# A decoder trunk's mixer: two 64-token halves in one product, decay levels by halves, one product for the upper scores

## Chip, cores and metric

The kernel runs on one core of a Trainium2 chip. The metric is the device time of one execution in microseconds (us); the median of three runs before the change is 965.5 us (965.27 to 966.09). The core's engines work side by side and meet through semaphores: PE (matrix products; PEld are its loads of the stationary operand), DVE (elementwise), ACT (activations and copies), POOL (small helper operations), and SP, which issues the DMAs.

## What is computed

The input is x, 256 tokens of 1024 values. Two layers follow each other. A layer is a half-step gated FFN, a token mixer, and a second half-step FFN, each with a residual and a layer norm. The mixer has two groups: trailing means over 2, 4, 8 and 16 tokens, and a gated linear recurrence (HGRN2) of four heads with 128 dimensions. The change concerns the recurrence:

```python
log_f = jnp.logaddexp(jnp.log(lb), jnp.log1p(-lb) + jax.nn.log_sigmoid(f_raw))
k = (1.0 - lb) * jax.nn.sigmoid(-f_raw)
# per head, state S (128 x 128), token t:
#   S_t = diag(f_t) S_{t-1} + (1 - f_t) outer v_t ;  o_t = S_t^T q_t
# within a chunk, with b = cumsum(log_f) over its tokens:
rel = b[:, :, :, None, :] - b[:, :, None, :, :]
decay = jnp.exp(jnp.where(causal, rel, -jnp.inf))
scores = jnp.einsum('bhtd,bhsd,bhtsd->bhts', q_c, k_c, decay)
o_intra = jnp.einsum('bhts,bhsv->bhtv', scores, v_c)
```

The score of two tokens s < t is thus a sum over the 128 dimensions of q times k times a decay of that dimension, and the decay is exp of the sum of the log gates between s and t.

## The kernel before

The 256 tokens are two halves of 128 (`hf` 0 and 1). Each weight arrives as fp32, is cast to a rounded high part on ACT and reduced to a low part on DVE (`halves`, L101), and a product of two fp32 operands is three products of parts (`mm3`, L95). In the FFN, `GT` (L282) makes the products with the high parts 512 columns wide and those with the low parts of the weights 256 columns wide.

The order on PE is written out: PE runs in program order (L88), and the small products of the mixer are dealt in between the large projections by `later`, a queue whose clock ticks once for each `mm3`. `later(n, fn)` issues `fn` n ticks on. ACT, DVE and POOL are ordered by the planner, by priority; the casts and subtractions of weights have a priority lowered by 400 (`BEHIND`), so they fill gaps.

The mixer (L519) projects five blocks (gate f, q, v, output gate, pooling input) for both halves in turn. For the recurrence:

- `post_f` (L542) turns the projected gate into log gates `ls` (128 tokens x 512 dimensions) and splits them into high and low parts `lh` and `ll` on all 128 tokens (L560 to L563).
- `decays(hf, h)` (L619), one call a head, forms sums of log gates over spans of tokens as products with a constant 0/1 matrix `cumM` of 1024 columns a half: for each of two groups of 512 columns one product with `lh` (L629) and one with `ll` (L630), accumulated in one PSUM bank, then an exponential on ACT into the tile `E` (L631).
- With the second head of a pair, DVE multiplies the decays by transposed q or k (`kT`, `qT`), 14 operations by `mul` (L637) and a copy of every second q on POOL (L636). Two of the 14 write `A256`, the operands of the product that joins the two halves of 128 tokens (`cross`).
- `grams(hf, hp)` (L651), one call a pair of heads, multiplies the decayed k by the decayed q: blocks of 128, 32 and 8 tokens, each cut into four quarters, three cuts a level, and a further operand for neighbouring tokens. For each level and head there is one fp32 product (L657). Its valid parts go into the tile `scores`, a part of `Pm`: three copies on ACT for the level of 128 (L665), masked copies on DVE for 32 and 8 (L668, L671). Fp32 products appear as two instructions each in the trace.
- `output` (L689) multiplies the scores by v.

After `post_q` of a half, its transposes come four ticks on; `decays` of head h follows at `lag + 2h` ticks, `grams` at `lag + 9` and `lag + 14`, and `cross` at `lag + 17`, with `lag` 7 in layer 0 and 11 in layer 1 (L584 to L590). The PSUM pool `psa` has four banks, which `decays` and `grams` share.

The constants come from `_constants` (L807) and are loaded once, in the first FFN (`load_consts`, L216).

Of the kernel before, what the change touches and what calls it, by code (L numbers as in the profile page):

```python
# [28 lines left out]
ALPHA = (2.0 * DEPTH) ** 0.25  # L29
LN_EPS = 1e-5  # L30
RMS_EPS = 1e-6
S32, FAR, S128, M128, M32, S8, M8, ODD = 0, 128, 224, 320, 512, 704, 832, 1024
WINDOWS = (2, 4, 8, 16)
PAD = 16
WOUT_ORDER = (4, 5, 6, 7, 0, 1, 2, 3)
# [39 lines left out]
def trunk(ctx: ExitStack, tc: tile.TileContext, t, out: bass.AP):  # L75
    nc = tc.nc
    pool = lambda name, bufs, **kw: ctx.enter_context(tc.tile_pool(name=name, bufs=bufs, **kw))
    cp = pool("const", 1)
    rawp = pool("raw", RAW)
# [6 lines left out]
    psa = pool("psa", 4, space=PSUM)  # L86
# [14 lines left out]
    def halves(dst_h, dst_l, src):  # L101
        first = nc.scalar.copy(dst_h, src)  # L102
        return first, nc.vector.tensor_tensor(dst_l, src, dst_h.bitcast(F32), ALU.subtract)  # L103
# [105 lines left out]
    la = cp.tile([P, 512], F32, name="la")  # L209
# [5 lines left out]

    def load_consts():  # L216
        for j in range(2):
            cm = rawp.tile([P, 1024], F32, name="raw")
# [300 lines left out]
    def mixer(l, win, wout):  # L519
        guard, mp = scoped("mix")  # L520
# [10 lines left out]
        lf, kn, qn, v, sg, u, mt = ([None, None] for _ in range(7))  # L531
# [10 lines left out]
        def post_f(hf, ps):  # L542
            f = mp.tile([P, 512], F32, name="tA", bufs=2)
            nc.scalar.copy(f, ps)
            tmp = mp.tile([P, 512], F32, name="tB", bufs=2)
            ls = mp.tile([P, 512], F32, name="tC", bufs=2)
            log_sigmoid(ls, f, tmp)
            if l > 0:
                nc.vector.tensor_tensor(ls, ls, lm, ALU.add)
            kn[hf] = mp.tile([P, 512], F32, name="kn")  # L550
            nc.vector.tensor_tensor(f, ls, f, ALU.subtract)
            nc.scalar.activation(kn[hf], f, AF.Exp)
            if l > 0:
                nc.vector.tensor_tensor(tmp, ls, la, ALU.subtract)
                nc.vector.tensor_tensor(ls, ls, la, ALU.max)
                nc.scalar.activation(tmp, tmp, AF.Abs)
                nc.scalar.activation(tmp, tmp, AF.Exp, scale=-1.0)
                nc.scalar.activation(tmp, tmp, AF.Ln, bias=1.0)
                nc.vector.tensor_tensor(ls, ls, tmp, ALU.add)
            lh = mp.tile([P, 512], F32R, name="lh", bufs=2)  # L560
            ll = mp.tile([P, 512], F32R, name="ll", bufs=2)
            halves(lh, ll, ls)
            lf[hf] = (lh, ll)  # L563

            def go():
                kT[hf] = flip(kn[hf], "kT")
            later(13, go)
# [37 lines left out]

        Es = [[None, None], [None, None]]

        def blocked(a, n):
            return a.rearrange("p j (n b) -> p j n b", n=n)

        def spans():

            for off, B in ((M128, 128), (M32, 32), (M8, 8)):
                for q in range(3):
                    w, n = (3 - q) * B // 4, P // B
                    yield B, n, q, off, n * w, slice((q + 1) * B // 4, B)
                    off += n * w

        def decays(hf, h):  # L619
            lh, ll = lf[hf]  # L620
            hp, j = h // 2, h % 2
            if j == 0:
                Es[hf][hp] = mp.tile([P, 2, ODD + 64], F32, name="E", bufs=2)
            E = Es[hf][hp]
            hs = slice(h * P, (h + 1) * P)
            for c in range(2):
                pe = psa.tile([P, 512], F32, name="acc")
                cs = slice(c * 512, c * 512 + 512)
                nc.tensor.matmul(pe, lh[:, hs], cumM[:, hf, cs], start=True, stop=False)  # L629
                nc.tensor.matmul(pe, ll[:, hs], cumM[:, hf, cs], start=False, stop=True)  # L630
# [5 lines left out]
            nc.gpsimd.tensor_copy(E[:, :, ODD:], q[:, :, 1::2])  # L636
            mul = lambda dst, a, b: nc.vector.tensor_tensor(dst, a, b, ALU.mult)  # L637
            e = E[:, :, S128:M128]
            mul(e, e, k[:, :, 0:96])
            for _, n, _, off, size, ts in spans():  # L640
                e = blocked(E[:, :, off:off + size], n)
                mul(e, e, blocked(q, n)[:, :, :, ts])
            e32 = blocked(E[:, :, S32:FAR], 4)
            side = (k, q)[hf]
            mul(blocked(far, 4)[:, :, :, 24:32], e32[:, :, :, 24:32], blocked(side, 4)[:, :, :, 24:32])
            mul(blocked(far, 4)[:, :, :, 0:24], blocked(E[:, :, FAR:S128], 4), blocked(side, 4)[:, :, :, 0:24])
            mul(e32[:, :, :, 0:24], e32[:, :, :, 0:24], blocked(k, 4)[:, :, :, 0:24])
            e = E[:, :, S8:M8]
            mul(e, e, k)

        def grams(hf, hp):  # L651
            E = Es[hf][hp]
            scores = Pm[hf][:, 2 * hp:2 * hp + 2, :]
            ps = {B: psa.tile([P, 2, w], F32, name="acc") for B, w in ((128, 192), (32, 192), (8, 256))}
            for B, rows, s0, t0 in ((128, 96, S128, M128), (32, P, S32, M32), (8, P, S8, M8)):
                for j in range(2):
                    nc.tensor.matmul(ps[B][0:rows, j, :], E[:, j, s0:s0 + rows], E[:, j, t0:t0 + ps[B].shape[2]],  # L657
                                     start=True, stop=True)
            first = {128: M128, 32: M32, 8: M8}
            m = 0  # L660
            for B, n, q, off, size, ts in spans():
                src = ps[B][:, :, off - first[B]:off - first[B] + size]
                if B == 128:
                    rows = slice(32 * q, 32 * q + 32)
                    nc.scalar.copy(scores[rows, :, ts], src[rows])  # L665
                else:
                    mask = blocked(masks[:, m:m + 2 * size].rearrange("p (j c) -> p j c", j=2), n)
                    nc.vector.copy_predicated(blocked(scores, n)[:, :, :, ts], mask, blocked(src, n))  # L668
                    m += 2 * size
            mask = masks[:, m:m + 128].rearrange("p (j c) -> p j c", j=2)  # L670
            nc.vector.copy_predicated(scores[:, :, 1::2], mask, ps[8][:, :, 192:256])  # L671

        def cross():
            px = psa.tile([P, NH, P], F32, name="acc")
# [99 lines left out]
        for hf in range(2):  # L774
# [31 lines left out]

def _constants():  # L807
    i = np.arange(P)
    s, tt = i[:, None], i[None, :]
    side = lambda q: (s > tt) & (s < (tt // q + 1) * q)  # L810
    parts, masks = {}, []
    for B in (128, 32, 8):
        q, parts[B] = B // 4, []
        for a in range(3):
            cols = i[i % B >= (a + 1) * q][None, :]
            ref = cols // B * B + (a + 1) * q
            parts[B].append((s >= ref) & (s <= cols))
            if B < 128:
                masks += 2 * [(s // B == cols // B) & (s % B // q == a)]
    masks += 2 * [s + 1 == i[None, 1::2]]  # L820
    cum = np.zeros((P, 2, 1024), np.float32)
    for hf, far in enumerate((s > tt, s <= tt)):
        last = i % 32 >= 24
        cum[:, hf] = np.concatenate([np.where(last, far, side(8)), far[:, ~last], side(32)[:, 0:96]]
                                    + parts[128] + parts[32] + [side(2)] + parts[8], axis=1)
    masks = np.concatenate(masks, axis=1).astype(np.float32)
# [51 lines left out]
```

## Time and profile before

| | |
|---|---|
| median of 3 runs | 965.5 us |
| profiled execution | 967.36 us |
| its span, first to last instruction | 965.6 us |
| PE busy | 955.1 us |
| PEld busy | 806.1 us |
| DVE busy | 653.3 us |
| ACT busy | 519.6 us |
| POOL busy | 27.8 us |
| HBM read | 178.76 MB |
| mean granted TensorE clock | 0.998 |

The page gives busy times of the engines, the span in 40 slices, and groups of instructions. In a row of groups, the names are line, engine, operation, written and read tiles, shapes and count; behind the bar stand the busy time in us and the mean of one in ns, and then the idle time of the engine just before, with what ended it. In a row of the timeline, the first number is the start in us from the span's start, the second the time to the end of the last instruction of the row. Products on PE are pipelined: one starts before the one ahead has ended, so starts and not durations tell what a product costs in a sequence. In the row of a stretch (from:to), there stand its length, the busy times of PE, PEld, DVE, ACT and POOL with their counts, the granted clock, the share of DMA and its GB/s. The mixers lie at about 180 to 290 us and 665 to 785 us.

### The profile page before, as it was taken

How to read it: one execution, taken by the hardware profiler on the slowest of the kernel's cores; microseconds unless marked ns; L12 is line 12 of the kernel's file. 1: busy time of each engine (PE TensorE's matmuls, PEld its weight loads, DVE VectorE, ACT ScalarE, POOL GpSimd, SP SyncE). 2: the span in 40 equal slices, each digit the busy share in tenths (PEclk: the TensorE clock that was granted, in tenths of full speed). 3: DMA queues.
4: the chain of work that ended last, by engine and by line, in shares of the span. 5: the costliest groups of instructions: out<-in, count | busy, mean ns of one | idle time of the engine just before them, and what ended most of it. 6: DMA issues, size and time to landing. Idle time of an engine off the chain costs nothing.

```text
span 965.6 us, 13125 instructions
## 1 busy us (share of the span) xinstructions
PE 955.1 (99%) x4817; PEld 806.1 (83%) x4817; DVE 653.3 (68%) x1092; ACT 519.6 (54%) x805; POOL 27.8 (3%) x50
## 2 busy tenths in 40 slices
PE   9999999999999999999999999999999999999996
PEld 7888888888887888888888888888888888888885
DVE  6876655769689775656676565647897897565625
ACT  6766544376455655454445645533965466645420
POOL 0000000010010000000000000000001000000000
PEclk9999999999999999999999999999999999999999
DMA  8967775343427876565346766543434377766301
GB/s 314 338 243 259 265 236 175 98 127 122 161 93 233 309 224 237 180 211 165 121 160 238 235 211 211 171 150 98 131 132 157 106 268 281 236 212 209 125 1 44
DMA packets 50801, 180.68 MB, mean 187 GB/s; under 512 B 6192, under 2 KB 6192, under 8 KB 50736
## 3 DMA queue, kind: packets, MB, share of 16 engines
q1 hardware_dynamic: 50544, 179.31, 55.0%
q8 instruction: 38, 0.62, 0.3%
q0 software_dynamic: 192, 0.53, 0.2%
q14 instruction: 27, 0.22, 0.1%
HBM read 178.76 MB, written 1.05 MB: 186 GB/s over the span
## 4 chain that ended last, share of the span: by engine, by line
PE 64%; DVE 2%; DMA 2%; ACT 1%; issue 1%; DVEq 0%; SPq 0%; ACTq 0%
PE gu L300 28%; PE acc L98 7%; PE acc L96 7%; PE acc L97 7%; PE gu L98 4%; PE gu L97 4%; PE gu L96 4%; DMA raw<-in_dn 1%; DMA raw<-in_gu 1%; PE acc L657 1%; DVE wl L103 1%; PE gu L177 1%; PE acc L630 0%; PE acc L629 0%; PE gu L406 0%
## 5 line engine op out<-in xcount | busy, mean ns | idle before, releaser
L102 ACT CAST wh<-raw 128x1024 fp32r<-128x1024 f32 x196 | 205.1, 1051 | 110.2 <-DMA raw<-in_gu 40.9
L103 DVE TENSOR_TENSOR wl<-raw,wh 128x1024 fp32r<-128x1024 f32 x196 | 235.6, 1218 | 23.3 <-ACT wh L102 11.6
L300 PE MATMUL gu<-xt,wh 128*128 128x512 f32 x768 | 180.6, 391 | 0.0
L103 DVE TENSOR_TENSOR dl<-raw,dh 128x1024 fp32r<-128x1024 f32 x88 | 106.6, 1223 | 95.9 <-ACT dh L102 95.8
L300 PEld LDWEIGHTS gu<-xt,wh 128*128 128x128 f32 x768 | 144.1, 188 | 31.5
L102 ACT CAST dh<-raw 128x1024 fp32r<-128x1024 f32 x88 | 91.5, 1050 | 103.0 <-DMA raw<-in_dn 99.2
L96 PE MATMUL acc<-dh,hth 128*128 128x512 f32 x352 | 140.0, 398 | 0.0
L98 PE MATMUL acc<-dh,htl 128*128 128x512 f32 x352 | 138.2, 393 | 0.0
L97 PE MATMUL acc<-dl,hth 128*128 128x512 f32 x352 | 137.6, 391 | 0.1
L96 PE MATMUL gu<-wh,xt 128*128 128x512 f32 x320 | 128.7, 402 | 0.0
L98 PE MATMUL gu<-wh,xt 128*128 128x512 f32 x320 | 125.3, 392 | 0.0
L97 PE MATMUL gu<-wl,xt 128*128 128x512 f32 x320 | 125.1, 391 | 0.0
L300 PE MATMUL gu<-xt,wl 128*128 128x256 f32 x768 | 99.6, 282 | 0.0
L300 PEld LDWEIGHTS gu<-xt,wl 128*128 128x128 f32 x768 | 96.8, 191 | 1.9
L323 DVE TENSOR_TENSOR sil<-gu,sil 128x256 f32<-128x256 f32 x64 | 26.9, 421 | 96.2 <-ACT sil L322 96.1
L98 PEld LDWEIGHTS acc<-dh,htl 128*128 128x128 f32 x352 | 66.1, 188 | 14.9 <-DVE htl L103 0.2
L97 PEld LDWEIGHTS acc<-dl,hth 128*128 128x128 f32 x352 | 66.2, 188 | 13.5 <-DVE dl L103 1.1
L96 PEld LDWEIGHTS acc<-dh,hth 128*128 128x128 f32 x352 | 66.2, 188 | 12.2 <-ACT hth L102 0.3
L98 PEld LDWEIGHTS gu<-wh,xt 128*128 128x128 f32 x320 | 60.1, 188 | 13.0
L97 PEld LDWEIGHTS gu<-wl,xt 128*128 128x128 f32 x320 | 60.2, 188 | 12.0
L96 PEld LDWEIGHTS gu<-wh,xt 128*128 128x128 f32 x320 | 60.2, 188 | 11.8
L300 PE MATMUL gu<-xt,xh 128*128 128x512 f32 x256 | 62.5, 396 | 0.0
(172 smaller groups left out, 1052.2 us busy)
## 6 DMA issues: line engine op xcount, KB each, us to landing
raw<-in_gu SPq DMA_DIRECT2D x172, 512.0 KB, 4.4
raw<-in_dn SPq DMA_DIRECT2D x88, 512.0 KB, 4.5
raw<-in_win SPq DMA_DIRECT2D x40, 512.0 KB, 4.1
raw<-in_wout SPq DMA_DIRECT2D x16, 512.0 KB, 4.1
lng<-in_ln_g SPq DMA_DIRECT2D x6, 512.0 KB, 4.5
lnb<-in_ln_b SPq DMA_DIRECT2D x6, 512.0 KB, 5.8
raw<-in_first SPq DMA_DIRECT2D x5, 384.0 KB, 6.0
x<-in_first SPq DMA_DIRECT2D x3, 384.0 KB, 8.0
```

The source lines that it names most:

```text
L96: nc.tensor.matmul(ps, lh, wh, start=start, stop=False)
L97: nc.tensor.matmul(ps, lh, wl, start=False, stop=False)
L98: nc.tensor.matmul(ps, ll, wh, start=False, stop=stop)
L102: first = nc.scalar.copy(dst_h, src)
L103: return first, nc.vector.tensor_tensor(dst_l, src, dst_h.bitcast(F32), ALU.subtract)
L177: nc.tensor.transpose(pt[:, k - a, :], self.nat[:, k * P:(k + 1) * P], ident)
L300: nc.tensor.matmul(ps[i][part][:, 2 * S - w:], weight.parts[lo][:, c:c + P], x[:, 0:w], start=kt == 0 and not lo, stop=kt == KT - 1 and lo ...
L323: nc.vector.tensor_tensor(dst, p[:, 0:S], dst, ALU.add)
L657: nc.tensor.matmul(ps[B][0:rows, j, :], E[:, j, s0:s0 + rows], E[:, j, t0:t0 + ps[B].shape[2]], start=True, stop=True)
```

## The change

The log gates of 128 tokens are no longer split into two tiles of 128 tokens. Two tiles `la` and `lb` hold 64 tokens each: the 128 rows of `la` are the high parts of tokens 0 to 63 and then the low parts of the same tokens, those of `lb` are the low parts of tokens 64 to 127 and then their high parts. The constant matrix is repeated for both, so one product sums high and low. `cumM` shrinks from 1024 columns a half to 576 a group of 64 tokens.

Each column of decays now needs one 64-token half alone. `decays` makes two tiles: `EA` (2 heads x 640) and `EB` (4 groups of head and 64 tokens x 256), by four products of 256 columns a head and two exponentials of 512. The levels of 32 and 8 tokens use sums inside 64 tokens. Sums that reach over the other half are made on DVE, by a multiplication with a scalar column (`whole`). The former level of 128 becomes one middle cut at token 64 and a cut in the middle of each 64; the three share one product of 128 x 128 (`upper`).

```diff
-            lh = mp.tile([P, 512], F32R, name="lh", bufs=2)
-            ll = mp.tile([P, 512], F32R, name="ll", bufs=2)
-            halves(lh, ll, ls)
-            lf[hf] = (lh, ll)
+            lf[hf] = [mp.tile([P, 512], F32R, name=n, bufs=2) for n in ("la", "lb")]
+            first, second = slice(0, 64), slice(64, P)
+            for part, here, there in zip(lf[hf], (first, second), (second, first)):
+                nc.scalar.copy(part[here], ls[here])
+                nc.vector.tensor_tensor(part[there], ls[here], part[here].bitcast(F32), ALU.subtract)
...
         def decays(hf, h):
...
-            for c in range(2):
-                pe = psa.tile([P, 512], F32, name="acc")
-                cs = slice(c * 512, c * 512 + 512)
-                nc.tensor.matmul(pe, lh[:, hs], cumM[:, hf, cs], start=True, stop=False)
-                nc.tensor.matmul(pe, ll[:, hs], cumM[:, hf, cs], start=False, stop=True)
-                nc.scalar.activation(E[:, j, cs], pe, AF.Exp)
+            own = EB.rearrange("p (j c) w -> p j c w", j=2)[:, j]
+            for dst, first in ((EA[:, j, 0:512].rearrange("p (c w) -> p c w", c=2), 64 * hf), (own, 320)):
+                pe = psa.tile([P, 2, 256], F32, name="acc")
+                for c in range(2):
+                    nc.tensor.matmul(pe[:, c, :], lf[hf][c][:, hs], cumM[:, c, first:first + 256], start=True, stop=True)
+                nc.scalar.activation(dst, pe, AF.Exp)
...
-            nc.gpsimd.tensor_copy(E[:, :, ODD:], q[:, :, 1::2])
...
+            mul(far[:, :, ts[near]], both[:, :, near, fars:fars + 64], side[:, :, ts[near]])
+            whole = c1[:, :, top + 63:top + 64] if hf == 0 else c0[:, :, fars + 63:fars + 64]
+            for i in range(2):
+                nc.vector.scalar_tensor_tensor(far[:, i, ts[other]], both[:, i, other, fars:fars + 64], whole[:, i, :],
+                                               side[:, i, ts[other]], ALU.mult, ALU.mult)
+            mul(halved(EA[:, :, 512:640]), both[:, :, :, top + 128:top + 192], halved(k))
+            low, up = halved(k)[:, :, :, 0:32], halved(q)[:, :, :, 32:64]
+            mul(halved(EA[:, :, top + 128:top + 192]), strided(EA, top, 320), low)
+            mul(halved(EA[:, :, top + 320:top + 384]), strided(EA, top + 32, 320), up)
+            mul(c0[:, :, top + 64:top + 128], c0[:, :, top + 64:top + 128], k[:, :, 0:64])
+            mul(c1[:, :, top:top + 64], c1[:, :, top:top + 64], q[:, :, 64:128])
+            k, q = by_halves(k), by_halves(q)
+            mul(halved(EA[:, :, 384 * hf:384 * hf + 128]),
+                EB[:, :, S32:S32 + 64].rearrange("p (j c) w -> p j c w", j=2), k.rearrange("p (j c) w -> p j c w", j=2))
+            nc.gpsimd.tensor_copy(EB[:, :, S32:S32 + 32], q[:, :, 1::2])
+            for _, n, off, size, t in spans():
+                e = blocked(EB[:, :, off:off + size], n)
+                mul(e, e, blocked(q, n)[:, :, :, t])
...
         def grams(hf, hp):
...
+            upper = psa.tile([P, 2, P], F32, name="acc")
+            ps = {B: psa.tile([P, 4, w], F32, name="acc") for B, w in ((32, 96), (8, 128))}
+            for j in range(2):
+                nc.tensor.matmul(upper[:, j, :], EA[:, j, top + 64:top + 192], EA[:, j, top + 256:top + 384],
+                                 start=True, stop=True)
+            for B, s0, t0 in ((32, 384 * hf, M32), (8, 512, M8)):
+                w = ps[B].shape[2]
                 for j in range(2):
+                    nc.tensor.matmul(ps[B][:, 2 * j:2 * j + 2, :], EA[:, j, s0:s0 + P], EB[:, 2 * j:2 * j + 2, t0:t0 + w],
                                      start=True, stop=True)
+            nc.scalar.copy(scores[0:64, :, 64:128], upper[0:64, :, 0:64])
+            for c in range(2):
+                nc.scalar.copy(scores[64 * c:64 * c + 32, :, 64 * c + 32:64 * c + 64],
+                               upper[64 + 32 * c:96 + 32 * c, :, 64 + 32 * c:96 + 32 * c])
...
-    cumM = cp.tile([P, 2, 1024], F32R, name="cumM")
+    cumM = cp.tile([P, 2, 576], F32R, name="cumM")
```

The masked copies keep their number and widths. The slots of `later`, the PSUM pool, the projections and the FFNs are as before.

More of the change, by code (lines that the diff above doesn't have):

```diff
@@ L217, in load_consts @@
         for j in range(2):
-            cm = rawp.tile([P, 1024], F32, name="raw")
+            cm = rawp.tile([P, 576], F32, name="raw")
             late_dma(cm, t["cumM"][:, j, :])
@@ L606, in mixer, with by_halves @@
         Es = [[None, None], [None, None]]
+        def by_halves(a):
+            return a.rearrange("p j (c t) -> p (j c) t", c=2)
         def blocked(a, n):
@@ L611, in spans @@
         def spans():
[L613 removed]
+            for off, B in ((M32, 32), (M8, 8)):
                 for q in range(3):
[L615 to L616 removed]
+                    w, n = (3 - q) * B // 4, 64 // B
+                    yield B, n, off, n * w, slice((q + 1) * B // 4, B)
                     off += n * w
         def decays(hf, h):
[L620 removed]
             hp, j = h // 2, h % 2
             if j == 0:
[L623 to L624 removed]
+                Es[hf][hp] = (mp.tile([P, 2, 640], F32, name="EA", bufs=2), mp.tile([P, 4, 256], F32, name="EB", bufs=2))
+            EA, EB = Es[hf][hp]
             hs = slice(h * P, (h + 1) * P)
[L626 to L631 removed]
+            own = EB.rearrange("p (j c) w -> p j c w", j=2)[:, j]
[4 more added lines that the diff above has]
+                nc.scalar.activation(dst, pe, AF.Exp)
             if j == 0:
@@ L644, in decays @@
-            side = (k, q)[hf]
[L645 to L649, printed above, removed]
+            halved = lambda a: a.rearrange("p j (c w) -> p j c w", c=2)
+            top, fars = (64, 0) if hf == 0 else (0, 192)
@@ new lines, in decays @@
+            c0, c1 = EA[:, :, 0:256], EA[:, :, 256:512]
+            both = halved(EA[:, :, 0:512])
+            side = (k, q)[hf]
+            near, other = (1, 0) if hf == 0 else (0, 1)
+            ts = [slice(0, 64), slice(64, P)]
+            mul(far[:, :, ts[near]], both[:, :, near, fars:fars + 64], side[:, :, ts[near]])
[3 more added lines that the diff above has]
+                                               side[:, i, ts[other]], ALU.mult, ALU.mult)
@@ new lines, in decays, with strided @@
+            k, q = by_halves(k), by_halves(q)
[5 more added lines that the diff above has]
+                mul(e, e, blocked(q, n)[:, :, :, t])
+        def strided(EA, first, step):
+            e = EA[:, :, first:first + 32]
+            return bass.AP(e.tensor, e.offset, [list(d) for d in e.ap[:-1]] + [[step, 2], list(e.ap[-1])])
@@ L651, in grams @@
         def grams(hf, hp):
-            E = Es[hf][hp]
+            EA, EB = Es[hf][hp]
             scores = Pm[hf][:, 2 * hp:2 * hp + 2, :]
-            ps = {B: psa.tile([P, 2, w], F32, name="acc") for B, w in ((128, 192), (32, 192), (8, 256))}
-            for B, rows, s0, t0 in ((128, 96, S128, M128), (32, P, S32, M32), (8, P, S8, M8)):
+            top = 64 if hf == 0 else 0
+            upper = psa.tile([P, 2, P], F32, name="acc")
+            ps = {B: psa.tile([P, 4, w], F32, name="acc") for B, w in ((32, 96), (8, 128))}
@@ L658, in grams @@
                                      start=True, stop=True)
-            first = {128: M128, 32: M32, 8: M8}
-            m = 0
[L661 to L669, printed above, removed]
@@ L673, in cross @@
+            m = 0
+            for B, n, off, size, t in spans():
+                off -= M32 if B == 32 else M8
+                src = ps[B][:, :, off:off + size]
+                nc.vector.copy_predicated(blocked(scores, n)[:, :, :, t], blocked(mask[:, :, m:m + size], n), blocked(src, n))
+                m += size
+            nc.vector.copy_predicated(scores[:, :, 1::2], mask[:, :, m:m + 32], ps[8][:, :, 96:128])
         def cross():
@@ L808, in _constants @@
     i = np.arange(P)
[L809 to L826, printed above, removed]
+    cum, masks = [], []
+    for c in range(2):
+        s = np.tile(64 * c + np.arange(64), 2)[:, None]
+        t = (64 * c + np.arange(64))[None]
+        until = lambda cols, end: (s > cols) & (s < end)
+        since = lambda cols, begin: (s >= begin) & (s <= cols)
+        side = lambda q: until(t, (t // q + 1) * q)
+        middle = [until(t[:, 0:32], 64 * c + 32), since(t[:, 32:64], 64 * c + 32)]
+        top = [since(t, 64)] + middle if c else middle + [until(t, 64)]
+        parts = []
+        for B in (32, 8):
+            for q in range(3):
+                cols = t[:, t[0] % B >= (q + 1) * B // 4]
+                parts.append(since(cols, cols // B * B + (q + 1) * B // 4))
+                masks.append((c, (i[:, None] // B == cols // B) & (i[:, None] % B // (B // 4) == q)))
+        masks.append((c, i[:, None] + 1 == t[:, 1::2]))
+        cum.append(np.concatenate([s > t] + top + [side(2)] + [s <= t] + parts + [side(8)], axis=1))
+    cum = np.stack(cum, axis=1).astype(np.float32)
+    masks = np.concatenate([m for _ in range(2) for _, m in masks], axis=1).astype(np.float32)
     w = np.array(WINDOWS, np.float32)[None, :, None]
```

13 lines of the change are left out of this document (3 added, 10 removed).

## Prediction

> **What bounds the kernel now.** I read the page's busy times and slices first, then the waits of PE, then the PE timeline inside the mixer.
>
> ```profile
> span 965.6 us, 13125 instructions
> PE 955.1 (99%) x4817; PEld 806.1 (83%) x4817; DVE 653.3 (68%) x1092; ACT 519.6 (54%) x805; POOL 27.8 (3%) x50
> PE   9999999999999999999999999999999999999996
> PEclk9999999999999999999999999999999999999999
> PE gu L375 <- DVE zero L372: 1.1, 1, 1.1
> PE gu L406 <- DVE hn L334: 0.9, 2, 0.7
> ```
>
> PE is busy in every slice but the last, at full granted clock, and its largest waits are about 1 us in the whole span. A busy matmul row is modelled, though, and rows overlap, so I price a product by the distance from its start to the next start. What counts is then simple: every start-to-start interval taken off PE shortens the run, unless PE, arriving earlier, finds its operands late.
>
> **The products of the decays.** Before, one call of `decays` issues four products of 512 columns (L629, L630); after, four of 256 columns, as high and low parts of 64 tokens share the 128 rows. The loads of the stationary operand stay four of 128 columns. Calls: 4 heads x 2 halves x 2 layers = 16, so 64 products.
>
> ```profile
> L629 PE MATMUL acc<-cumM,lh 128*128 128x512 f32 x32 | 12.6, 392 | 0.0
> L630 PE MATMUL acc<-cumM,ll 128*128 128x512 f32 x32 | 12.6, 392 | 0.0
> L629 PEld LDWEIGHTS acc<-cumM,lh x32: 187/187/188, 210.9 to 719.0; 128*128 128x128 f32 x32
> 211.17 0.39 PE L629 MATMUL acc<-cumM,lh 128*128 128x512 f32 x1
> ...
> 211.86 0.40 PE L630 MATMUL acc<-cumM,ll 128*128 128x512 f32 x1
> 212.09 0.39 PE L96 MATMUL gu<-wh,xt 128*128 128x512 f32 x1
> 335.68 1.10 PE L300 MATMUL gu<-xt,xl 128*128 128x256 f32 x8
> 336.62 1.12 PE L300 MATMUL gu<-xt,wl 128*128 128x256 f32 x8
> 337.58 1.10 PE L300 MATMUL gu<-xt,xl 128*128 128x256 f32 x8
> 338.52 1.12 PE L300 MATMUL gu<-xt,wl 128*128 128x256 f32 x8
> 339.47 0.40 PE L96 MATMUL acc<-dh,hth 128*128 128x512 f32 x1
> ```
>
> The four of 512 take 212.09 - 211.17 = 0.92 us, 0.230 each. The FFN has products of exactly the new kind (same type, 256 columns, a new stationary operand each time): 32 of them from 335.68 to 339.47 take 3.79 us, 0.118 each. Four make 0.474. Saved: 0.446 a call, times 16 = **7.1 us**. From below, if the load (187 ns, the PEld row) were not hidden at all, four would take 0.75 and 16 calls save 2.7. From above, an exact half (0.115) saves 7.4.
>
> **The products of the scores.** These are full fp32; each appears as two instructions. A call of `grams` (8 of them) has 12 instructions: four of 192 columns for the 128-level, four of 192 and four of 256. After, the first four have 128 columns; the others keep their widths, read in two pieces.
>
> ```profile
> L657 PE MATMUL acc<-E 128*128 128x256 f32 x32 | 8.2, 379 | 0.0
> L657 PE MATMUL acc<-E 128*128 128x192 f32 x32 | 6.5, 326 | 0.0
> L657 PE MATMUL acc<-E 128*96 128x192 f32 x32 | 6.5, 324 | 0.0
> 221.10 2.32 PE L657 MATMUL acc<-E 128*96 128x192 f32 x12
> 223.26 0.60 PE L572 MATMUL gu<-ident,tA 128*128 128x128 f32 x4
> 252.54 1.05 PE L693 MATMUL acc<-v,Pm 128*128 128x128 f32 x8
> 253.35 0.48 PE L96 MATMUL gu<-wh,xt 128*128 128x512 f32 x1
> 253.66 0.40 PE L97 MATMUL gu<-wl,xt 128*128 128x512 f32 x1
> ```
>
> The call takes 223.26 - 221.10 = 2.16. Eight fp32 instructions of 128 columns and one product of 512 take 253.66 - 252.54 = 1.12, less 0.23 leaves 0.89, 0.111 each. A line through both (12a + 2560b = 2.16, a + 128b = 0.111) gives b = 0.00081 us a column, so 192 columns cost 0.163. Saved: 4 x 0.052 = 0.21 a call, **1.7 us** in eight. Bounds: 0 (if pieces of the moving operand cost what narrowing gains) and 2.0 (0.81/8 for 128 columns).
>
> PE alone would thus lose 7.1 + 1.7 = 8.8 us. Its granted clock is already full, so nothing comes or goes there.
>
> **What is added beside PE.** In `post_f` one cast and one subtraction on 128 partitions become two of each on 64, of the same width; the nearest price is the whole one.
>
> ```profile
> L103 DVE TENSOR_TENSOR ll<-tC,lh 128x512 fp32r<-128x512 f32 x4 | 2.7, 687 | 0.1
> L102 ACT CAST lh<-tC 128x512 fp32r<-128x512 f32 x4 | 2.5, 630 | 0.8 <-DVE tC L508 0.8
> 216.72 0.35 DVE L637 TENSOR_TENSOR E<-E,kT 128x192 f32<-128x192 f32 x1
> 216.99 1.91 DVE L637 TENSOR_TENSOR E<-E,qT 128x192 f32<-128x192 f32 x9
> 218.81 0.49 DVE L637 TENSOR_TENSOR A<-E,kT 128x64 f32<-128x64 f32 x2
> 219.21 0.96 DVE L637 TENSOR_TENSOR E<-E,kT 128x192 f32<-128x192 f32 x3
> 701.36 0.95 DVE L637 TENSOR_TENSOR E<-E,kT 128x192 f32<-128x192 f32 x3
> 702.65 2.32 PE L657 MATMUL acc<-E 128*96 128x192 f32 x12
> 237.70 0.68 DVE L637 TENSOR_TENSOR E<-E,kT 128x192 f32<-128x192 f32 x2
> 241.07 2.32 PE L657 MATMUL acc<-E 128*96 128x192 f32 x12
> 719.25 0.69 DVE L637 TENSOR_TENSOR E<-E,kT 128x192 f32<-128x192 f32 x2
> 721.74 2.32 PE L657 MATMUL acc<-E 128*96 128x192 f32 x12
> 687.00:732.00 45.00, 45.00 (x216) 37.99 (x215) 42.87 (x116) 33.94 (x58) 1.30 (x2) 1.00 0.46 152
> ```
>
> So 0.6 to 0.7 us more on DVE and on ACT for each half of each layer, four times. The multiplications of a pair of heads go from 14 DVE operations to 15, over the same 2048 elements of a partition. Fourteen took from 216.72 to about 219.9 (the last of the three at 219.21 is already the next pair's), 3.2 us; nine narrow ones took 1.82, 0.20 each, so one more makes 3.4. In all DVE gains 4 x 0.65 + 8 x 0.2 = 4.2 us. The exponentials keep number and width, the masked copies too, and the three copies of the top level stay three. The constants lose 0.46 MB of DMA and part of two casts in the first FFN, which PE does not wait for. No DMA is moved past another on SP. The POOL copy of q (L636) now overwrites columns that DVE must have read, so it is issued after a DVE operation instead of ahead of all; behind it on POOL stand only the pooling group's small copies and the powers of the norms.
>
> All this is hidden as long as PE does not arrive first at `grams`. That cover is the thin place. With `later` counting slots, the first `grams` of a half follows four calls of `decays`, so it comes 4 x 0.446 = 1.8 us earlier, while its own last decay product comes only 0.9 earlier. In layer 0 (first half) E is complete at the latest at 219.21 + 0.96 = 220.17, PE arrives at 221.10; in layer 1 at 702.31 against 702.65. DVE runs without a gap ahead of both, so I let its work start no earlier, and the extra half operation (0.6) and the fifteenth (0.2) push it later. The new order helps: the top product needs 8 of 15 operations, the 32-level 12, the 8-level 15. Layer 0: these are ready at about 219.1, 220.0 and 220.7; PE asks for them at 219.3, 219.8 and 220.4: a stall of 0.3. Layer 1: all ready by 702.9, the last asked for at 702.65 - 1.8 + 0.44 + 0.65 = 701.9: at most 1.0, and nothing if ACT's exponentials come forward with PE. The first calls of the second halves have more room (E done at 238.4 and 719.9, `grams` at 241.07 and 721.74), but DVE is busy 42.87 of the 45 us from 687 to 732, which shrink to about 40.6 while DVE's work grows to 43.8. What does not fit, 3.2 us, can be put off only in the form of weight subtractions (L103), which have a low priority. I take **1.0 us** of stalls in all, between 0 and 4.4 (3.2, the 1.0 of layer 1's first call, and 0.2 of layer 0's window).
>
> Sum against the profiled execution (967.36 us, its span 965.6 and 1.8 around it): 967.4 - 8.8 + 1.0 = 959.6. The median of the runs shown, 965.5, is 1.9 lower, so the forecast is 957.7.
>
> **One rule against it.**
>
> ```profile
> L636 POOL COPY E<-qT 128x128 f32<-128x128 f32 x8 | 4.4, 561 | 70.9 <-ACT qT L574 42.2 <-DVE E L637 18.2 <-PE acc L657 10.5
> ```
>
> The eight copies take 0.56 us on average, now mostly away from DVE's multiplications. After the change each stands in the middle of them. If DVE stood still for each copy, a pair would take 3.4 + 0.56 = 4.0 us; with the stalls above growing by up to that in the four first calls (one for each half of a layer), 4 x 0.56 = 2.2 more, 959.9. The Trainium skill, "SBUF — State Buffer", section "Who interferes with whom", states that a VectorE instruction with two SBUF inputs and a GpSimd instruction that reads SBUF exclude each other, and the later one waits for the whole of the earlier. No row of this trace settles who would wait here.
>
> **The rivals.**
> - *DVE queue.* PE waits at `grams` for what DVE could not put off: the full 4.4 us, so 965.5 - 8.8 + 4.4 = 961.1. For it: DVE's 42.87 of 45. Against: the waits of PE name no weight subtraction in the mixer today, so these have room to be put off.
> - *POOL in the middle*, as above: 959.9.
> - *The loads show.* At 0.188 a product the gain is 2.7 + 1.7 = 4.4: 961.1. Against it: the 32 products from 335.68, with as many loads, ran at 0.118.
> - *Slower: the new multiplications are slow.* They walk two strided pieces, four blocks or a scalar column; if such patterns ran at half speed, a pair would take 6.8 us, 3.6 more than today's 3.2. Room from the end of E to the first `grams` of a half, less the 0.9 that PE gains on it: 0.3 and 1.8 us in layer 0 (219.9 to 221.10, 238.4 to 241.07), -0.3 and 0.9 in layer 1 (702.0 to 702.65, 719.9 to 721.74), together 2.7. The four calls would stall 4 x 3.6 - 2.7 = 11.7, more than the 8.8 gained: 965.5 + 2.9 = 968.4. It decides from 2.9 us more a pair, a pair of 6.1. Against it: the nine operations at 216.99 are already blocked patterns and run at 0.20 each.
>
> **How the numbers follow.** Forecast 0.71, DVE queue 0.12, POOL 0.06, loads 0.04, slow multiplications 0.07. The range: 955.8 (7.4 + 2.0 and no stall, 956.1, and 0.3 for the runs' spread) to 961.4 (the first and third rival with the same 0.3). About 0.2% of the time, 1.9 us, is what a measurement can tell from no change. Faster: all but the last rival, 0.93; of the last, 0.03 lands within 0.2% and 0.04 is slower.
>
> **What would show it.** Right: decay products of 256 columns, four in 0.47 us start to start; 12 instructions of `grams` in 1.95; PE busy time down by 8 to 9 us and its span with it; a few tenths of us between the last product ahead of the first `grams` of a half and the `grams`, above all in layer 1. Wrong: PE waits on E or EB of a us and more, in several calls; four decay products in 0.7 us or more; a pair's multiplications well over 3.4 us; a POOL copy that ends after DVE's last multiplication. A change in the FFN stretches would be none of my steps.

## The result and the profile after

The changed kernel takes 959.19 us in the median (five runs, 958.18 to 959.67), the one before 965.53 (five runs, 965.27 to 966.48). The ratio is 0.9928 with a 95% interval of 0.9917 to 0.9938: faster by 6.0 to 8.0 us. The forecast was 957.7 in a range of 955.8 to 961.4. The profiled execution of the changed kernel took 958.23 us.

These are the page's lines that answer to those of before.

```profile
span 956.5 us, 13129 instructions
...
PE 946.6 (99%) x4817; PEld 800.0 (84%) x4817; DVE 654.8 (68%) x1104; ACT 519.6 (54%) x809; POOL 32.4 (3%) x50
...
PEclk9999999999999999999999999999999999999999
```

PE has as many instructions as before and 8.5 us less of busy time (955.1 to 946.6); the span fell by 9.1, more than the medians, since the profiled execution of the kernel before was a long one. DVE and POOL gained a little, ACT nothing. The kernel is still bound by PE, at full clock. Next the groups of the changed products in the changed kernel, by shape (busy time and mean ns behind the bar).

```profile
L634 PE MATMUL acc<-cumM,lb 128*128 128x256 f32 x32 | 8.3, 280 | 0.0
L634 PE MATMUL acc<-cumM,la 128*128 128x256 f32 x32 | 8.2, 278 | 0.0
L681 PE MATMUL acc<-EA 128*128 128x128 f32 x32 | 5.0, 277 | 0.1
```

They are 64 products of 256 columns where 64 of 512 stood, and 32 of 128 where 32 of 192 stood. What they cost is read from the PE timeline (start, length, line, tiles, number of instructions; a wait and what ended it in brackets): one call of `decays`, the first call of `grams` in layer 0, and a call without a wait.

```profile
210.97 0.28 PE L634 MATMUL acc<-cumM,la 128*128 128x256 f32 x1
...
211.44 0.39 PE L96 MATMUL gu<-wh,xt 128*128 128x512 f32 x1
...
218.83 0.39 PE L98 MATMUL gu<-wh,xt 128*128 128x512 f32 x1
219.36 0.68 PE L681 MATMUL acc<-EA 128*128 128x128 f32 x4
220.31 1.99 PE L686 MATMUL acc<-EB,EA 128*128 128x192 f32 x8 [0.26 <-DVE EB L640]
222.14 0.60 PE L574 MATMUL gu<-ident,tA 128*128 128x128 f32 x4
...
226.46 0.61 PE L681 MATMUL acc<-EA 128*128 128x128 f32 x4
...
228.24 0.58 PE L96 MATMUL gu<-wh,xt 128*128 128x512 f32 x1
```

Four decay products take 211.44 - 210.97 = 0.47 us, where four took 0.92. An undisturbed call of `grams` takes 228.24 - 226.46 = 1.78 up to the start of a wide projection; the like distance before was 1.97 (from 227.60 to 229.57). The two reductions are 16 x 0.45 = 7.2 and 8 x 0.2 = 1.6, together 8.8.

The four rows from 218.83 are the other side. From the last projection (218.83) to the first score product (219.36) pass 0.53 us, where 0.23 is usual: 0.30 of waiting. The four top products need 0.45 and have 0.95 up to the next group at 220.31: a wait of 0.42 ahead of the level of 32 is most of the difference. The rest of the call, 220.31 to 222.14, holds another of 0.14 ahead of the level of 8. Behind each of the three the first product is slower by 0.07 to 0.10 (the four of 128 columns are 0.68 long here, 0.61 in the call without a wait). In all 1.1 us are given back in this one call. What PE waited for stands on the DVE and POOL timelines of the same stretch.

```profile
215.69 0.69 DVE L565 TENSOR_TENSOR la<-tC,la 64x512 fp32r<-64x512 f32 x1
...
216.59 0.28 DVE L640 TENSOR_TENSOR A<-EA,kT 128x128 f32<-128x128 f32 x1
216.89 0.69 DVE L565 TENSOR_TENSOR lb<-tC,lb 64x512 fp32r<-64x512 f32 x1
217.59 0.48 DVE L652 SCALAR_TENSOR_TENSOR A<-EA,kT 128x64 f32<-128x64 f32 x2
217.99 0.82 DVE L640 TENSOR_TENSOR EA<-EA,kT 128x256 f32<-128x256 f32 x3
218.73 0.49 DVE L640 TENSOR_TENSOR EA<-EA,qT 128x128 f32<-128x128 f32 x2
219.13 0.35 DVE L640 TENSOR_TENSOR EB<-EB,qT 128x192 f32<-128x192 f32 x1
219.40 0.42 DVE L640 TENSOR_TENSOR EA<-EB,kT 128x256 f32<-128x256 f32 x1
219.74 1.03 DVE L640 TENSOR_TENSOR EB<-EB,qT 128x128 f32<-128x128 f32 x5
220.68 0.29 DVE L640 TENSOR_TENSOR A<-EA,kT 128x128 f32<-128x128 f32 x1
...
219.98 1.13 POOL L664 COPY EB<-qT 128x128 f32<-128x128 f32 x1 [26.09 <-DVE EA L640]
```

The top operands are complete at 218.73 + 0.49 = 219.22, and the top products start at 219.36. The copy on POOL ends at 219.98 + 1.13 = 221.11, and the 8-level starts right after it. The subtractions of `la` and `lb` for the other half, which nobody needs for another 10 us, stand ahead of the pair's multiplications (`la`, 215.69) and in the middle of them (`lb`, 216.89); each takes DVE 0.70 us up to the next start.

### The profile page after: what moved, and what is told of

It reads as the page before. It is cut to its first block, busy times and chain, and to the rows that moved or that the text cites. A ratio compares the mean times of both kernels' runs of the same rounds, so it can differ in the third digit from the quotient of the medians.

```text
span 956.5 us, 13129 instructions
## 1 busy us (share of the span) xinstructions
PE 946.6 (99%) x4817; PEld 800.0 (84%) x4817; DVE 654.8 (68%) x1104; ACT 519.6 (54%) x809; POOL 32.4 (3%) x50
```

## Experiments

The table has the median of each kernel, but for two that stand below it (`split_grams`, `split_pool`), and the waits of PE in its profiled execution, in us; the kernel before took 965.5 to 965.6 in the same jobs. A wait is the distance from one start to the next, less the usual distance for that kind of product; in the mixers the slower first product behind a wait is counted with it.

| kernel | median | waits in the mixers | waits where an FFN begins |
|---|---|---|---|
| before, three profiles | 965.5 | 0, 0, 0 | 2.5, 1.1, 2.0 |
| changed, two profiles | 959.2, 959.0 | 1.4, 1.9 | 1.2, 1.0 |
| later_grams | 958.3 | 1.3 | 1.3 |
| split_late, two profiles | 957.2, 957.6 | 0.4, 0.5 | 0.8, 1.8 |
| double_decays | 964.3 | 0 | 0.7 |
| pool_early | 959.6 | 1.8 | 1.8 |
| wide_upper | 959.4 | 1.5 | 1.8 |
| split_gu | 956.4 | 0.1 | 0.3 |

**The changed kernel again** (`again`, no edit).

> The changed kernel once more, for its spread and a second profile. Theory (products of fewer columns save 8.7 us on PE, about 1.1 us of it is given back where PE waits in the mixer, the rest of the spread comes from waits at the start of the FFNs): 958 to 960 us, and again 0.8 to 1.0 us of waiting in the first call of grams in layer 0. Rival (the waits in the mixer are chance): that call's 12 products follow each other without a gap this time.

Measured: 959.04 us, ratio 0.9929 (0.9916 to 0.9941). The first call of `grams` waits 0.30, 0.42 and 0.14 us again, to the hundredth, so that wait is no chance. A second one, 0.2 us in the first profile, is now 0.7: the third product of the last `grams` in layer 1. The DVE timeline of that place in this run, and PE's in a second fence:

```profile
718.79 1.22 DVE L103 TENSOR_TENSOR wl<-raw,wh 128x1024 fp32r<-128x1024 f32 x1
719.93 0.22 DVE L698 COPY_PREDICATED Pm<-masks,acc 128x64 f32<-128x64 uint8 x1
720.06 1.22 DVE L103 TENSOR_TENSOR wl<-raw,wh 128x1024 fp32r<-128x1024 f32 x1
```

```profile
718.93 0.82 PE L686 MATMUL acc<-EB,EA 128*128 128x192 f32 x4
720.30 1.10 PE L686 MATMUL acc<-EB,EA 128*128 128x256 f32 x4 [0.55 <-DVE Pm L698]
```

The operands were long there. PE waits for a masked copy of the call before (L698, ending at 720.15). I read it as the PSUM bank that this copy empties; `split_gu` below tests that. Between the masked copies, each of which needs the one ahead of it, the planner has set weight subtractions of 1.2 us.

**The decay products twice** (`double_decays`): PE's columns of before, all else as after the change.

```diff
+                    for _ in range(2):
-                    nc.tensor.matmul(pe[:, c, :], lf[hf][c][:, hs], cumM[:, c, first:first + 256], start=True, stop=True)
+                        nc.tensor.matmul(pe[:, c, :], lf[hf][c][:, hs], cumM[:, c, first:first + 256], start=True, stop=True)
```

> Each product of the decays is issued twice into the same place, so PE does as many columns in decays as before the change, while DVE, ACT and POOL do what they do in the changed kernel. Theory (PE is the bound all through the mixer and the number of columns is the gain): 64 more products of 0.118 us, 7.5 us slower than the changed kernel, less the 0.9 us of waiting that PE no longer finds: 965 to 966.5 us. Rival (the mixer is partly bound by DVE, or the gain came from DVE's or POOL's new order): less than 4 us slower than the changed kernel.

Measured: 964.26 us, 5.2 above `again` (ratio 0.9985, 0.9975 to 0.9994). A call takes 0.95 us again, and every wait in the mixers is gone. 64 x 0.118 = 7.5, less the 1.4 to 1.9 of waits, is 5.6 to 6.1. The measured 964.26 lies 0.7 below the range that was expected, and well over the rival's 4. From the kernel before, 965.6 in this job, the narrower score products (1.6) come off and 16 x 0.03 for the slightly longer calls comes on, which makes 964.5. So most of the gain is PE's columns, and the order on the other engines brought none that shows.

**The first grams two slots later** (`later_grams`).

```diff
-                later(lag + 9, lambda: grams(hf, 0))
+                later(lag + 11, lambda: grams(hf, 0))
```

> The first call of grams of each half comes two slots (about 1.4 us) later, nothing else. Theory (PE arrives there before DVE is ready): the 0.87 us of waiting in layer 0 goes, the time falls by 0.6 to 1.0 us against the changed kernel. Rival (PE would wait for the same work anyhow, the wait only moves to the second call of grams, to cross or to output): the same time within 0.3 us, with a new gap on PE behind it.

Measured: 958.3 us, 0.7 less than `again`, with ratio intervals that overlap (0.9906 to 0.9933 here). The wait in the first call of layer 0 is gone, as the theory has it. But the two calls of a half now stand closer, and waits of 0.6 and 0.3 us for masked copies appear in layer 1, and one of 0.2 in layer 0's last call, as the rival has it in kind. A moved call pays in another resource.

**The split of the second half's log gates put back** (`split_late`).

```diff
             for part, here, there in zip(lf[hf], (first, second), (second, first)):
-                nc.scalar.copy(part[here], ls[here])
-                nc.vector.tensor_tensor(part[there], ls[here], part[here].bitcast(F32), ALU.subtract)
+                with tc.high_priority(offset=-100 * hf):
+                    nc.scalar.copy(part[here], ls[here])
+                    nc.vector.tensor_tensor(part[there], ls[here], part[here].bitcast(F32), ALU.subtract)
```

> The splitting of the second half's log gates into la and lb gets a priority lowered by 100, so on DVE both subtractions (0.69 us each) stand behind the multiplications of both pairs of heads of the first half in layer 0, no longer between them. Theory (the queue of DVE is what PE waits for in the first grams): E is ready 1.2 us earlier, the 0.87 us of waiting goes, 0.6 to 1.0 us less than the changed kernel. Rival (the copy on POOL or the exponentials on ACT are what it waits for): the waiting stays above 0.5 us.

Measured: 957.19 us (ratio 0.9912, 0.9898 to 0.9925), 1.9 less than `again` on the same chip; the two intervals still overlap, so the trace has to carry the argument. The timeline of layer 0's first `grams` in this kernel, first DVE, then PE, then POOL:

```profile
215.08 0.48 DVE L652 SCALAR_TENSOR_TENSOR A<-EA,kT 128x64 f32<-128x64 f32 x2
...
221.61 0.69 DVE L565 TENSOR_TENSOR lb<-tC,lb 64x512 fp32r<-64x512 f32 x1
...
218.20 0.61 PE L681 MATMUL acc<-EA 128*128 128x128 f32 x4
218.65 1.68 PE L686 MATMUL acc<-EB,EA 128*128 128x192 f32 x8
220.16 0.60 PE L574 MATMUL gu<-ident,tA 128*128 128x128 f32 x4
...
217.46 1.15 POOL L664 COPY EB<-qT 128x128 f32<-128x128 f32 x1 [24.40 <-DVE EA L640]
```

The scalar operations start 2.5 us earlier (217.59 to 215.08). Of that, 0.86 is only that this whole execution is ahead: PE reaches the call at 218.20, and without its wait of 0.30 it would have been 219.06 in the changed kernel. The remaining 1.65 are the two subtractions, 0.70 each, and a little besides. `lb` follows behind both pairs, and the products run without a gap, although the copy on POOL is as long as before (1.15). The pair's last exponential on ACT ends at 214.32 here and at 215.18 in the changed kernel, the same 0.86, so ACT did not come forward. So DVE's queue was what PE waited for, and in it the two half-height subtractions. From 218.20 to 220.16 the call takes 1.96 us, from 219.36 to 222.14 it took 2.78: with the 0.30 ahead of it that is the 1.1. The median shows 1.9; this run's profile has also 0.4 less of the bank wait and 0.2 less where FFNs begin than `again`'s, and the rest is within the spread of its runs (956.2 to 959.1). A second time (`split_again`) it took 957.6.

> split_late once more, to be compared with split_gu on the same chip: 956.8 to 957.8 us, and one wait in the mixers, of 0.3 us, in layer 1.

Measured: 957.6 us (ratio 0.9916, 0.9902 to 0.993), with one wait in the mixers of 0.4 us in layer 1.

**The copy on POOL with columns of its own** (`pool_early`): `EB` 288 wide, the constants' columns in another order, and the copy issued ahead of DVE's multiplications.

```diff
-            nc.gpsimd.tensor_copy(EB[:, :, S32:S32 + 32], q[:, :, 1::2])
+            nc.gpsimd.tensor_copy(EB[:, :, ODD:ODD + 32], by_halves(q)[:, :, 1::2])
```

> The copy of every second q gets columns of its own (EB 288 wide instead of 256), so POOL makes it ahead of DVE's multiplications as before the change. Theory (DVE keeps its pace beside the copy and the copy is the one that waits, so it costs PE only the third and smallest wait of the first grams): the copies shorten from 1.14 us on average to under 0.7, the third wait (0.14 us) goes, the two waits ahead of it (0.30 and 0.42) stay; 0 to 0.3 us less than the changed kernel. Rival (the copy and DVE exclude each other both ways, and DVE loses its time too): a pair's 15 multiplications become 0.3 us or more shorter each, the first two waits shrink as well, 0.7 us or more less.

Measured: 959.56 us (four runs, 957.34 to 961.03; ratio 0.9935, 0.9921 to 0.9949). The groups of the copy, first in the changed kernel and then here:

```profile
L664 POOL COPY EB<-qT 128x128 f32<-128x128 f32 x8 | 9.1, 1138 | 87.7 <-DVE EA L640 87.7
```

```profile
L642 POOL COPY EB<-qT 128x128 f32<-128x128 f32 x8 | 4.0, 509 | 68.2 <-ACT qT L576 42.1 <-DVE EA L640 16.8 <-DVE Pm L603 5.1
```

And DVE's timeline in this kernel:

```profile
217.25 0.48 DVE L653 SCALAR_TENSOR_TENSOR A<-EA,kT 128x64 f32<-128x64 f32 x2
...
220.34 0.29 DVE L640 TENSOR_TENSOR A<-EA,kT 128x128 f32<-128x128 f32 x1
```

The copies halve, the third wait goes, and the first two (0.30 and 0.42) stay. DVE's stretch from the scalar operation to the next pair takes 220.34 - 217.25 = 3.09 us without the copy beside it, and 220.68 - 217.59 = 3.09 with it: DVE loses nothing. The time shows no gain; this run had 0.8 us of the bank wait in layer 1.

**The upper product at its former width** (`wide_upper`).

```diff
-            upper = psa.tile([P, 2, P], F32, name="acc")
+            upper = psa.tile([P, 2, 192], F32, name="acc")
...
-                nc.tensor.matmul(upper[:, j, :], EA[:, j, top + 64:top + 192], EA[:, j, top + 256:top + 384],
+                nc.tensor.matmul(upper[:, j, :], EA[:, j, top + 64:top + 192], EA[:, j, top + 256:top + 448],
```

> The product of the upper levels reads 192 columns instead of 128 (the 64 further ones are used by nobody), the width that each product of the level of 128 had before. Theory (an fp32 instruction costs 0.052 us less for 64 columns less): 32 instructions, 1.7 us more on PE, of which up to 0.2 are hidden in the waits of the first grams: 1.4 to 1.7 us slower than the changed kernel, 960.5 to 960.9 us. Rival (the narrowing of the scores brought nothing, the width is hidden behind the loads): the same time, the call of grams as long as now.

Measured: 959.38 us (ratio 0.9934, 0.9921 to 0.9947). The PE timeline of an undisturbed call says what was expected:

```profile
226.69 0.82 PE L681 MATMUL acc<-EA 128*128 128x192 f32 x4
...
228.67 0.58 PE L96 MATMUL gu<-wh,xt 128*128 128x512 f32 x1
```

A call takes 228.67 - 226.69 = 1.98 us against 1.78, so eight cost 1.6 more. The median shows 0.2 to 0.3 of it against the changed kernel in other jobs. The intervals of the ratios (a microsecond each way) hold both, so the time decides nothing here; the width is shown on PE alone.

**The second grams later, too** (`split_grams`), and the same with POOL's copy early (`split_pool`).

```diff
-                later(lag + 14, lambda: grams(hf, 1))
+                later(lag + 16, lambda: grams(hf, 1))
...
-                    later(lag + 17, cross)
+                    later(lag + 18, cross)
```

> As split_late, and the second call of grams of each half comes two slots later (cross one slot later). Theory (in layer 1 the third product of the second half's second call waits 0.3 to 0.7 us for a PSUM bank, which masked copies of the call before free late, as weight subtractions stand between them on DVE): that wait goes, 0.3 to 0.5 us less than split_late: 956.5 to 957.0 us. Rival (it waits for EB or the POOL copy, or the wait moves to output): the wait stays or comes back at the products with v; the time of split_late within 0.2 us.

> split_grams and pool_early together. Theory (nothing waits for POOL once DVE is ready early): as split_grams within 0.3 us, 956.4 to 957.0 us. Rival (DVE's time beside the copies matters): 0.7 us or more below split_grams.

Measured: 961.29 us (0.9955, 0.9943 to 0.9967) and 961.03 us (0.9951, 0.9938 to 0.9964), both some 4 us slower than `split_late`: the theory of this step fell. Three views of `split_grams` in layer 1: PE's timeline, those of ACT and DVE, and stretches with the busy time of PE, PEld, DVE, ACT and POOL in turn, then the granted clock, DMA share and GB/s.

```profile
719.79 0.82 PE L686 MATMUL acc<-EB,EA 128*128 128x192 f32 x4
723.27 2.04 PE L686 MATMUL acc<-EB,EA 128*128 128x256 f32 x4 [2.67 <-POOL ms L730]
```

```profile
721.54 1.04 ACT L102 CAST wh<-raw 128x1024 fp32r<-128x1024 f32 x1 [1.04 <-DVE ms L728]
722.49 0.25 ACT L688 COPY Pm<-acc 64x128 f32<-64x128 f32 x1
722.75 0.42 ACT L690 COPY Pm<-acc 32x64 f32<-32x64 f32 x2
...
723.72 1.09 DVE L733 SCALAR_TENSOR_TENSOR y<-acc,ms,sg 128x128 f32<-128x128 f32 x4
```

```profile
720.30:723.30 3.00, 0.33 (x3) 0.07 (x2) 1.50 (x6) 1.81 (x5) 1.02 (x1) 0.92 0.96 365
723.30:725.50 2.20, 2.20 (x5) 1.79 (x6) 2.20 (x8) 0.00 (x0) 0.00 (x0) 0.50 0.56 229
725.50:728.00 2.50, 2.50 (x15) 2.19 (x14) 2.25 (x4) 1.48 (x2) 0.00 (x0) 0.86 0.37 75
```

Two slots on, the last `grams` of layer 1 comes behind `output` of the first half, which takes a bank of the same pool and holds it up to its four scalings (L733). But the third product does not wait for that bank: it starts at 723.27, and the scalings start at 723.72. Nor was it the power on POOL that the row names, which ends at 722.83. What ends just ahead of it, at 722.75 + 0.42 = 723.17, are ACT's copies (L688, L690) of the call's own first product; in `split_pool` the copies end at 722.80 and the product starts at 722.90. The account that fits is that with one bank held by `output` the call has to use its own first bank again, and the copies that empty it stand on ACT behind a weight cast that itself began only at 721.54. No row names the bank, and no run was made to test this. PE stands for 2.7 us, and then runs at half its clock (0.50) for 2.2 us and at 0.86 for 2.5 more: 2.2 x 0.50 + 2.5 x 0.14 = 1.4 lost besides. The 2.7 and the 1.4 are the 4 us.

**A bank from the other pool** (`split_gu`): `split_late` and

```diff
-            upper = psa.tile([P, 2, P], F32, name="acc")
+            upper = psg.tile([P, 2, P], F32, name="gu")
```

> As split_late, and the product of the upper levels takes its PSUM bank from the projections' pool instead of the pool that decays and grams share. Theory (the third product of the last grams in layer 1 waits for a bank that masked copies free late): with one bank less asked for in that pool the wait of 0.3 us goes, and nothing else changes: 0.2 to 0.5 us less than split_late in this job. Rival (the projections then wait for a bank of theirs, or the masked copies are waited for anyhow): gaps ahead of the projections of the mixer, the same time or more.

Measured: 956.41 us (five runs, 956.38 to 957.38; ratio 0.9906, 0.9892 to 0.992), 1.2 less than `split_again` in the same job, whose four runs lie all above (957.41 to 958.24). The ratios' intervals overlap. Expected were 0.2 to 0.5 less; the bank wait of `split_again`'s profile is 0.4, and the rest lies where the FFNs begin (0.3 against 1.8 in the two profiles), which the edit does not touch. The last `grams` of layer 1:

```profile
716.62 0.61 PE L681 MATMUL gu<-EA 128*128 128x128 f32 x4
717.07 1.68 PE L686 MATMUL acc<-EB,EA 128*128 128x192 f32 x8
718.66 1.13 PE L722 MATMUL acc<-v,Pm 128*128 128x128 f32 x8
```

The 8-level no longer waits: it starts 0.65 behind 717.07, at 717.72, though the third masked copy of the call before ends only at 718.52. So it was the bank. This kernel has the lowest median of all, and leaves 0.1 us of waits in the mixers.

**The kernel before, twice more** (`before_1`, `before_2`), to see how usual its first profile was.

> The kernel before once more, for a second profile: its first one was of an execution of 967.4 us, 1.9 above its median. Theory (the two kernels' spread is in the waits of PE at the very start and where an FFN begins, and the change does not touch it): no wait of PE inside the mixers, 0.5 to 1.5 us of waits where the FFNs begin instead of 2.3, a time of 965 to 966 us. Rival (the kernel before waits as much in its mixers as the changed one, in usual executions): gaps ahead of its score products.

> A third profile of the kernel before. Theory: as for before_1, no wait in the mixers, 0.5 to 1.5 us where the FFNs begin. Rival: waits of PE ahead of the score products, as in the changed kernel.

Measured: 966.05 and 966.74 us, one execution each. Neither has a wait in the mixers. Where the FFNs begin they wait 1.1 and 2.0 us (expected 0.5 to 1.5; the second is over it), so these waits change from run to run by a microsecond, and with them the time.

## Why the prediction was right, point by point

- **Decay products**: 0.474 us for four was worked out, 0.47 measured; 7.1 to 7.2 us. Taking the price from another product of the same shape was enough, and `double_decays` shows that the time follows PE's columns.
- **Score products**: 0.21 us a call was worked out, 0.20 measured.
- **The cover of DVE**: the total of 1.0 us was low (1.4 and 1.9 in the two profiles, of a possible 4.4), and its parts were wrong. The first call of layer 0 was priced at 0.3 and cost 1.1. I let one half subtraction push E back; both stood ahead of the multiplications that count, and the copy on POOL closed the call. The first call of layer 1, priced at up to 1.0, waits for nothing, since the planner set its pair of heads (from 691.38) ahead of the splitting (696.01). The 3.2 us that would not fit on DVE in layer 1 did not come as a wait for operands. (By the prediction's own prices DVE's work there grows by 0.65 + 4 x 0.2 = 1.45, not 0.9, so 3.7 would not fit; over the whole span DVE's busy time rose by 1.5 us, not by 4.2, and what became shorter was not followed up.) DVE is full there (40.46 of the 40.5 us from 683 to 723.5), but the weight subtractions that it put off come back as the wait for a PSUM bank, 0.2 to 0.8 us, which was not among my steps. One part was too low, one never came and one was not thought of, so that the total still lies within 0.4 to 0.9 us of the 1.0 is luck.
- **POOL**: of the rival's two halves one is true. The copies grew from 0.56 to 1.14 us, and DVE did not stand still for them: six of the eight slowed no DVE operation by more than 0.05 us, the other two one each by 0.1 (last section). On PE it cost 0.14 us, and the slower product behind, in one call. The Trainium skill, "SBUF — State Buffer", "Who interferes with whom", has the two exclude each other, the later one waiting for the whole of the earlier. The traces bear out that they exclude each other, but mostly it is the copy that waits, and for more than one operation.
- **The loads, slow multiplications**: from the scalar operations at 217.59 up to the next pair's first at 220.68 fourteen of the fifteen took 3.09 us, with one more of 0.2 it is 3.3, where 3.4 was worked out. The loads stayed hidden (0.118 a product).
- **The sum**: 7.8 us of gain were forecast. PE loses 8.8 and finds 1.4 to 1.9 of waits: 6.9 to 7.4 by the traces. The medians moved 6.3 and 6.5, the ratio's interval is 6.0 to 8.0. Whether the half microsecond or so between them is real stays open: waits at the FFNs differ by as much between executions of one kernel, and two or three profiles of each do not average them out.

## What to carry to other kernels

Where one engine is bound throughout, an edit that takes columns from it can be priced to a few per cent by start-to-start distances of a like product elsewhere in the same trace. What then decides the rest is who was covered by those columns: look at the queue order of the engine that feeds the shortened part, and move work that nobody needs yet behind the work that is now late. Before a call is moved to a later slot, see which call it is moved past, what that one holds, and what it puts into the queues ahead of the moved call.

## What the runs showed of the hardware

In `split_grams` a wait of 2.7 us on PE was enough to halve the granted clock (0.50 over the next 2.2 us), and cost half as much again behind it, while the waits below 1 us elsewhere left it at full. The clock fell before PE went on: 0.92 over the 3.00 us from 720.30 is half clock for the last 0.5 of them, which begins some 2.2 us after PE's last product ended (an estimate from these rows). In the traced execution of `split_pool` a wait of 2.98 us was followed by 0.50 for the 4.7 us from 722.90 to 727.60. It need not happen each time: of that kernel's six executions (959.12 to 962.56 us) the two of 959.12 and 959.52 have a mean clock of 0.998, like the changed kernel's (0.998 to 0.999), and the others 0.995 or 0.996. The Trainium skill, "TensorE: Matmul & The Clock Gate", "Why this matters for your kernels", asks for no gap over about 3 us, behind which the clock falls to half; the traces agree as to the fall, at gaps of 2.7 and 2.98 us.

A copy on POOL gives way to DVE for long. The POOL timeline of the changed kernel in layer 1, two copies of one shape, and DVE's of the six multiplications beside each and the weight subtraction behind:

```profile
710.76 0.30 POOL L664 COPY EB<-qT 128x128 f32<-128x128 f32 x1 [10.38 <-DVE EA L640]
714.19 2.38 POOL L664 COPY EB<-qT 128x128 f32<-128x128 f32 x1 [3.13 <-DVE EA L640]
...
710.54 1.40 DVE L640 TENSOR_TENSOR EB<-EB,qT 128x192 f32<-128x192 f32 x6
...
713.97 1.30 DVE L640 TENSOR_TENSOR EB<-EB,qT 128x192 f32<-128x192 f32 x6
715.18 1.22 DVE L103 TENSOR_TENSOR wl<-raw,wh 128x1024 fp32r<-128x1024 f32 x1
716.32 0.38 DVE L698 COPY_PREDICATED Pm<-masks,acc 128x192 f32<-128x192 uint8 x1
```

The first copy got in between two operations: it took 0.30, and DVE's six took 0.1 longer. The second found no gap. It took 2.38, past five multiplications and the whole subtraction, all with two inputs in SBUF, and ended in the masked copy, which reads PSUM (714.19 + 2.38 = 716.57); DVE's six went at their usual pace. Why one gets in and the other doesn't, no run was made to tell.
